# A hybrid attention and state-space layer: gate weights and decay rows loaded from GpSimd's queue, both directions' state products in one PSUM bank

## The chip, the cores and the metric

The kernel runs on one core of a Trainium2 chip. Its time is the device time of one execution in microseconds. Times are the median of several runs; the profile comes from one more execution. In the profile the engines are PE (TensorE matmul), PEld (TensorE weight load), DVE (VectorE), ACT (ScalarE), POOL (GpSimd) and SP (SyncE, which in this kernel issues every DMA).

## The reference

One layer on 512 latent tokens and 256 context tokens, width 2048, float32. Cut to what matters:

```python
shift, scale, gate = split(silu(c) @ w_mod + b_mod, 3)
px = (rmsnorm(x, norm_g) * (1 + scale) + shift) @ w_in     # latent
pc = (rmsnorm(ctx, norm_g) * (1 + scale_c) + shift_c) @ w_in
# attention: 16 heads of 64, 4 KV heads, window of 128 plus all context keys, sink, rotary
att = windowed_gqa(q, k, v, k_ctx, v_ctx, sink)
# state space: 16 heads of 64 in 4 groups, state 128, chunks of 128, forward and backward
u = silu(dwconv(xbc, conv_w, conv_b)); xs, B, C = split(u)
a_cs = cumsum(dt * a)                                       # per head and direction
y = (C B^T * exp(segsum(a_cs))) @ (dt * xs) + C @ state * exp(a_cs) + xs * d_skip
x = x + gate * concat(rmsnorm(att * silu(g)), rmsnorm(y * silu(z))) @ w_out
return rmsnorm(x, final_norm_g)
```

The vector `gate` (2048 numbers) is a product of one row, silu(c), with a 2048 x 2048 matrix. The states pass from chunk to chunk, from left to right for one direction and from right to left for the other; the context's final state is each direction's first.

## The kernel before, in words

Activations lie with the model width on the partitions, tokens along the free axis. Every projection is done in split precision: a weight tile is loaded as float32 (`wr`), ScalarE rounds it to `wh`, VectorE subtracts to get the rest `wl`, and TensorE adds three products (`mm` at L49 is the line of all of them). A unit is 128 output columns over 16 steps of k: `load_unit` loads it in two halves, each split in two quarters, and `proj` collects latent columns in the bank `pj` and, for units that context needs as well, context columns in `pjc`. Two buffers hold `wr`, four each hold `wh` and `wl`.

The stages in order: modulation and the z columns (to about 137 us), v and dt columns (to about 198), then units 1 to 16 in four groups of four (x, x, B, C columns of a state-space group), then k, q and g columns with attention (to about 861), then the output projection.

While the units of group g+1 run, the scan pieces of group g are put between their matmuls. `stream(g, i, mid)` gives `proj` a table of what to emit at which step k: `tokens(g)` at step 8 of the next group's first unit, `states(g)` after it, then `decay`, `state_term` and `back` for each pair of heads. The parts that matter here:

- `tokens` (L511): four matmuls give C B^T in a bank of the tag `tp`, VectorE makes the two masked copies `cb` from it (L521), and TensorE transposes xs and B into further `tp` banks (`xtp`, `btp`). The tag `tp` has two banks, so of three `xtp` in a row one needs the bank that `cb` reads.
- `states` (L544): for each of three steps and each of two directions, `xw` (VectorE), the product `stx` in a `tp` bank, and the update of `stt` on VectorE: first times `etot`, then plus the bank.
- `decay` (L574): for each head and direction the row of cumulated decays is broadcast from DRAM (`csd`) into `df` (four buffers; 128 partitions) and `ec` (two buffers; two heads of 64 partitions); ScalarE makes the exponentials, VectorE multiplies `df` with `cb`. `back` (L624) uses `df` in the product `yps`.
- `gate_step` (L280): the vector gate is computed on VectorE, 64 steps, one at each quarter of units 1 to 16. Step i multiplies a 128x512 weight tile `wg` with a column of silu(c) and adds it to `ga`. Weights are loaded two steps ahead into two buffers. After each 16 steps a matmul with ones sums over partitions, the row is stored to `grow`, and the only buffer of `ga` is set to zero by POOL (L289) for the next 16.

Instructions on each engine run in the order that a planner wrote at build time. It goes by program order, with blocks under `tc.high_priority` moved ahead by the number given, and by its own model of when an instruction is ready. `tc.issue_after(ld.ins)` orders an instruction behind the load `ld` on the same queue: the gate loads stand behind their unit's `wr` load on SP. A queue works in order: a load whose buffer is not free holds what stands behind it.

Of the kernel before, what the change touches and what calls it, by code (L numbers as in the profile page):

```python
# [14 lines left out]
P = 128  # L15
# [28 lines left out]
def emit(tc, xin, ctxT, wmod, wgate, bgate, wz, wvd, wu, wo, fng, vecs, cst, rope, out, dbg=None):  # L44
    nc = tc.nc
    es = ExitStack()

    def mm(o, l, r, start, stop):
        return nc.tensor.matmul(o, l, r, start=start, stop=stop)  # L49
# [4 lines left out]
    def tt(eng, o, a, b, op):  # L54
        eng.tensor_tensor(out=o, in0=a, in1=b, op=op)  # L55
# [7 lines left out]
    with es:  # L63
# [5 lines left out]
        def bank(tag, name, dt=F32, shape=(P, 512)):  # L69
            return ps.tile(list(shape), dt, tag=tag, name=name, bufs=pcount[tag])  # L70
# [200 lines left out]
        gacc, gw = [], []  # L271

        def gbuf(odd, name):
            if odd:
                return w2(name, "wg", 1)
            return wp.tile([P, 512], F32, tag="wg", name=name, bufs=GB)
# [3 lines left out]
        def gate_step(ld):  # L280

            i = next(gsteps, None)
            if i is None:
                return
            n, k = divmod(i, KT)
            if k == 0:
                ga = wp.tile([P, 512], F32, tag="ga", name=f"ga_{n}", bufs=1)
                gacc.append(ga)
                nc.gpsimd.memset(ga, 0.0)  # L289
                with tc.issue_after(ld.ins):  # L290
                    nc.sync.dma_start(ga[0:1, :], bgate[:, n * 512:(n + 1) * 512])
            ga = gacc[n]
            for ii in range(len(gw), min(i + 2, 4 * KT)):
                n_, k_ = divmod(ii, KT)
                gw.append(gbuf(ii % 2, f"wg_{n_}_{k_}"))
                with tc.issue_after(ld.ins):
                    nc.sync.dma_start(gw[ii], wgate[n_, k_])
            wg = gw[i]
            geng.scalar_tensor_tensor(out=ga, in0=wg, scalar=sc0[:, k:k + 1], in1=ga, op0=ALU.mult, op1=ALU.add)  # L299
            if k == KT - 1:  # L300
                gp = bank("tp", f"gp_{n}", shape=(1, 512))
                mm(gp, ones[:, 0:1], ga, True, True)
                nc.scalar.activation(ga[0:1, :], gp, AF.Copy)
                nc.sync.dma_start(grow[:, n * 512:(n + 1) * 512], ga[0:1, :])


        def load_unit(u, ctxp=False):

            for hf in range(2):
                with tc.high_priority(HP_W):  # L310
                    wr = wp.tile([P, 8, P], F32, tag="wr", name=f"wr_{u}_{hf}", bufs=WR)
                    ld = nc.sync.dma_start(wr, wu[u, :, hf * 8:hf * 8 + 8, :])
                for qf in range(2):
                    with tc.high_priority(HP_W):
                        wh = wp.tile([P, 4, P], F32R, tag="wh", name=f"wh_{u}_{hf}_{qf}", bufs=4)
                        rr = wr[:, qf * 4:qf * 4 + 4, :]
                        nc.scalar.activation(wh, rr, AF.Copy)  # L317
                        wl = wp.tile([P, 4, P], F32R, tag="wl", name=f"wl_{u}_{hf}_{qf}", bufs=4)
                        tt(nc.vector, wl, rr, f32(wh), ALU.subtract)
                    if 1 <= u < 17:  # L320
                        gate_step(ld)
                    for i in range(4):
                        yield hf * 8 + qf * 4 + i, wh[:, i, :], wl[:, i, :]

        def proj(u, with_ctx, mid=(), btag="mm"):

            a = bank("mm", f"pj_{u}")
            b = bank(btag, f"pjc_{u}", shape=(P, CT)) if with_ctx else None
            late = []
            for k, wh, wl in load_unit(u):  # L330
                s0, s1 = k == 0, k == KT - 1
                if k in mid:
                    mid[k]()
                mm(a, wh, xh[k], s0, False)
                mm(a, wh, xl[k], False, False)
                mm(a, wl, xh[k], False, s1)
                if with_ctx:
                    late.append((k, wh, wl))
                    if k % 4 == 3:
                        for kk, h, l in late:  # L340
                            mm(b, h, ch[kk], kk == 0, False)
                            mm(b, h, cl[kk], False, False)
                            mm(b, l, ch[kk], False, kk == KT - 1)
                        late = []
            return a, b
# [60 lines left out]
        z7, _ = proj(0, False)  # L406
# [12 lines left out]
        def w2(name, tag="w2", bufs=4, shape=(P, S)):  # L419
            return sd.tile(list(shape), F32, tag=tag, name=name, bufs=bufs)  # L420
# [4 lines left out]
        csd = dp.tile([32, S], F32, name="csd")  # L425
# [118 lines left out]
        def states(g):  # L544

            xtok, btok = G[g]["xtok"], G[g]["btok"]
            hs = slice(4 * g, 4 * g + 4)

            def xw(d, t):
                o = w2(f"xw_{g}_{d}_{t}", "xw", 2, (P, 4, HD))  # L550
                tt(nc.vector, o, xtok[:, t, :].rearrange("p (a b) -> p a b", a=4),
                   wdt[:, d, t, hs].unsqueeze(2).to_broadcast([P, 4, HD]), ALU.mult)
                return o.rearrange("p a b -> p (a b)")

            stt_ = [w2(f"stt_{g}_{d}", f"stt{d}", 1, (P, NT, 256)) for d in range(2)]
            for d in range(2):
                first = 0 if d == 0 else 3
                sp_ = bank("tp", f"stc_{g}_{d}", shape=(P, 256))
                mm(sp_, btok[:, 4, :], xw(d, 4), True, False)
                mm(sp_, btok[:, 5, :], xw(d, 5), False, True)  # L560
                nc.scalar.activation(stt_[d][:, first, :], sp_, AF.Copy)
            for stp in range(3):
                for d in range(2):
                    c = stp if d == 0 else 3 - stp
                    nx = c + 1 if d == 0 else c - 1
                    sp_ = bank("tp", f"stx_{g}_{d}_{c}", shape=(P, 256))
                    mm(sp_, btok[:, c, :], xw(d, c), True, True)
                    tt(nc.vector, stt_[d][:, nx, :].rearrange("p (a b) -> p a b", a=4),
                       stt_[d][:, c, :].rearrange("p (a b) -> p a b", a=4),
                       etot[:, d, c, hs].unsqueeze(2).to_broadcast([P, 4, HD]), ALU.mult)  # L570
                    tt(nc.vector, stt_[d][:, nx, :], stt_[d][:, nx, :], sp_, ALU.add)
            G[g]["stt"] = stt_

        def decay(g, pr):  # L574

            cb = G[g]["cb"]
            tix = 2 * g + pr
            ecs = [w2(f"ec_{tix}_{d}", "ec", 2) for d in range(2)]

            for d in range(2):  # L580
                with tc.high_priority(HB):
                    for hh in range(2):
                        nc.sync.dma_start(ecs[d][hh * 64:hh * 64 + 64], csd[d * 16 + tix * 2 + hh].partition_broadcast(64))
                nc.scalar.activation(ecs[d], ecs[d], AF.Exp)
            dm = []
            for hh in range(2):
                r = tix * 2 + hh
                dx = []
                for d in range(2):

                    df = w2(f"df_{r}_{d}", "df", DF)
                    with tc.high_priority(HB):
                        nc.sync.dma_start(df, csd[d * 16 + r].partition_broadcast(P))
                    for c in range(NT):
                        cc = slice(c * P, (c + 1) * P)
                        nc.scalar.activation(df[:, cc], df[:, cc], AF.Relu, bias=cs[:, d, c, r:r + 1], scale=-1.0)  # L596
                    nc.scalar.activation(df, df, AF.Exp, scale=-1.0)
                    for c in range(NT):
                        cc = slice(c * P, (c + 1) * P)
                        nc.scalar.activation(df[:, cc], df[:, cc], AF.Copy, scale=dtt[:, d, c, r:r + 1])  # L600
                    tt(nc.vector, df, df, cb[d], ALU.mult)
                    dx.append(df)
                tt(nc.vector, dx[0], dx[0], dx[1], ALU.add)
                dm.append(dx[0])
            G[g]["dec", pr] = dm, ecs
# [138 lines left out]
        for j in range(4):  # L744
            qs = []
            for i in range(2):
                a, _ = proj(U0 + 18 + 2 * j + i, False)
# [23 lines left out]
            for b in range(NT):  # L771
# [46 lines left out]
                for n, t in enumerate(kts):  # L818
                    tp = bank("tp", f"ptp_{j}_{b}_{n}")
# [18 lines left out]
            for jj in {0: (), 1: (0,), 2: (1,), 3: (2, 3)}[j]:  # L838
                for i in range(2):
                    t = 2 * jj + i  # L840
                    a, _ = proj(U0 + 26 + t, False)
# [233 lines left out]
```

## Time and profile before

| | |
|---|---|
| median of 3 runs | 1054.75 us (1053.28 to 1058.65) |
| the profiled execution | 1057.19 us, span 1055.4 us |
| granted TensorE clock, mean | 0.985 of full speed |
| busy: PE, PEld | 1012.8 us (96%), 818.6 us (78%) |
| busy: DVE, ACT, POOL | 693.2 us (66%), 538.6 us (51%), 141.4 us (13%) |
| gate weight loads `wg` | 64 of 256 KB, from SP |
| decay loads `df` and `ec` | 32 of 256 KB and 32 of 128 KB, from SP |
| unit weight loads `wr` | 70 of 512 KB, from SP |

"Busy" is the time in which an engine had an instruction under way; matmuls are pipelined, so a busy TensorE may still be short of its peak. A wait is idle time of an engine that ended when another one's instruction, or a DMA, released it. A row of the waits names the engine and line that waited, what released it, the total in microseconds, how many times, and the longest. A row of the order of time names start, duration, engine, line, the instruction, tiles as out<-in, and in brackets the idle time before it and its releaser.

### The profile page before, as it was taken

What the parts mean: (1) busy time and instruction counts of PE and PEld (TensorE: products, weight loads), DVE (VectorE), ACT (ScalarE), POOL (GpSimd) and SP (SyncE); (2) the same over time, 40 slices, a digit from 0 to 9 for tenths busy, and PEclk for the clock granted to TensorE, in tenths of its full rate; (3) what the DMA queues carried; (4) which work ended last, traced back from release to release, by engine and by line L of the source; (5) the groups of instructions that cost most, each with busy time, mean ns of one, the idle gap of its engine ahead of it and who ended that gap; (6) DMA issues with size and microseconds to landing.
All of it is one profiled execution on the core that took longest, in us unless ns stands there. A gap on an engine that the chain in (4) does not pass through costs nothing.

```text
span 1055.4 us, 15566 instructions
## 1 busy us (share of the span) xinstructions
PE 1012.8 (96%) x5682; PEld 818.6 (78%) x5682; DVE 693.2 (66%) x1346; ACT 538.6 (51%) x1236; POOL 141.4 (13%) x96
## 2 busy tenths in 40 slices
PE   5999999999999999999998899999999998999996
PEld 4676789888887787788876778777777777888885
DVE  4323378564875875775759888788797865333765
ACT  6222265255537637546645567575666654333333
POOL 0232300000000000000008000000000018644220
PEclk8999999999999999999999899999999998999999
DMA  9999964363534544534131211112111134442304
GB/s 330 383 343 348 341 213 124 101 196 110 170 121 150 160 130 150 157 122 141 61 106 60 80 41 61 41 40 81 40 60 56 45 142 187 141 167 88 106 29 160
DMA packets 53404, 147.31 MB, mean 140 GB/s; under 512 B 6056, under 2 KB 6568, under 8 KB 53072
## 3 DMA queue, kind: packets, MB, share of 16 engines
q1 hardware_dynamic: 53328, 146.31, 41.7%
q8 instruction: 45, 0.74, 0.3%
q14 instruction: 31, 0.25, 0.1%
HBM read 142.02 MB, written 4.27 MB: 139 GB/s over the span
## 4 chain that ended last, share of the span: by engine, by line
PE 59%; DVE 10%; DMA 8%; ACT 5%; issue 3%; POOL 1%; SPq 0%; ACTq 0%; DVEq 0%; POOLq 0%
PE pj L49 25%; PE o L49 14%; PE pjc L49 5%; PE pv L49 3%; PE ptp L821 3%; DMA wg<-in_wgate_dram 3%; PE sl L49 3%; DMA df<-csd 2%; DMA ec<-csd 2%; PE sc L49 2%; DVE wl L55 1%; DVE ga L299 1%; PE stx L49 1%; DVE df L55 1%; DVE ec L55 1%
## 5 line engine op out<-in xcount | busy, mean ns | idle before, releaser
L49 PE MATMUL pj<-xh,wl 128*128 128x512 f32 x560 | 225.7, 403 | 3.7 <-DVE wl L55 3.7
L49 PE MATMUL pj<-xh,wh 128*128 128x512 f32 x560 | 228.7, 408 | 0.5 <-ACT kT L701 0.5
L49 PE MATMUL pj<-xl,wh 128*128 128x512 f32 x560 | 226.0, 404 | 0.0
L317 ACT ACTIVATE wh<-wr 128x512 fp32r<-128x512 f32 x140 | 87.5, 627 | 125.0 <-PE pjc L49 79.0
L55 DVE TENSOR_TENSOR wl<-wr,wh 128x512 fp32r<-128x512 f32 x140 | 97.8, 700 | 43.6 <-ACT wh L317 42.8
L49 PEld LDWEIGHTS pj<-xh,wl 128*128 128x128 f32 x560 | 106.0, 189 | 26.2 <-DVE wl L55 4.6
L49 PEld LDWEIGHTS pj<-xh,wh 128*128 128x128 f32 x560 | 106.2, 190 | 23.8 <-ACT df L596 2.8
L49 PEld LDWEIGHTS pj<-xl,wh 128*128 128x128 f32 x560 | 106.1, 190 | 19.3
L55 DVE TENSOR_TENSOR wol<-wo,woh 128x512 fp32r<-128x512 f32 x56 | 54.3, 983 | 65.4 <-ACT woh L911 59.0
L55 POOL TENSOR_TENSOR hacc<-hacc,hsq 128x512 f32<-128x512 f32 x14 | 21.2, 1512 | 420.8 <-ACT hsq L719 420.6
L911 ACT ACTIVATE woh<-wo 128x512 fp32r<-128x512 f32 x56 | 34.7, 629 | 73.3 <-PE o L49 65.2
L299 DVE SCALAR_TENSOR_TENSOR ga<-wg,sc,ga 128x512 f32<-128x512 f32 x64 | 47.9, 748 | 36.5 <-DMA wg<-in_wgate_dram 36.3
L49 PE MATMUL pjc<-chq,wh 128*128 128x256 f32 x224 | 64.0, 286 | 0.7 <-DVE xs L487 0.7
L49 PE MATMUL pjc<-clq,wh 128*128 128x256 f32 x224 | 63.6, 284 | 0.0
L49 PE MATMUL pjc<-chq,wl 128*128 128x256 f32 x224 | 63.6, 284 | 0.0
L596 ACT ACTIVATE df<-df,cs 128x128 f32<-128x128 f32 x128 | 43.2, 391 | 29.1 <-DMA df<-csd 29.0
L825 ACT ACTIVATE ph<-ptp 128x512 fp32r<-128x512 f32 x72 | 41.1, 598 | 28.4 <-PE ptp L821 26.9
L49 PE MATMUL o<-woh,hsh 128*128 128x512 f32 x128 | 52.1, 407 | 3.1 <-ACT part L930 3.1
L55 DVE TENSOR_TENSOR pl<-ptp,ph 128x512 fp32r<-128x512 f32 x72 | 48.5, 684 | 8.2 <-ACT ph L825 8.0
L796 ACT ACTIVATE pe<-sl,nm 128x256 f32<-128x256 f32 (+1 forms) x64 | 33.7, 526 | 37.2 <-DVE nm L794 35.5
L49 PE MATMUL o<-wol,hsh 128*128 128x512 f32 x128 | 51.2, 400 | 0.0
L49 PE MATMUL o<-woh,hsl 128*128 128x512 f32 x128 | 51.1, 399 | 0.0
(274 smaller groups left out, 2296.4 us busy)
## 6 DMA issues: line engine op xcount, KB each, us to landing
wr<-in_wu_dram SPq DMA_DIRECT2D x70, 512.0 KB, 3.7
wm<-in_wmod_dram SPq DMA_DIRECT2D x64, 512.0 KB, 7.7
wg<-in_wgate_dram SPq DMA_DIRECT2D x64, 256.0 KB, 2.8
wo<-in_wo_dram SPq DMA_DIRECT2D x32, 512.0 KB, 4.8
df<-csd SPq DMA_DIRECT2D x32, 256.0 KB, 4.1
wsr<-in_wz_dram SPq DMA_DIRECT2D x16, 448.0 KB, 6.8
wr_v<-in_wvd_dram SPq DMA_DIRECT2D x16, 288.0 KB, 2.9
xt<-in_xin_dram SPq DMA_DIRECT2D x8, 512.0 KB, 8.4
```

The source lines that it names most:

```text
L49: return nc.tensor.matmul(o, l, r, start=start, stop=stop)
L55: eng.tensor_tensor(out=o, in0=a, in1=b, op=op)
L299: geng.scalar_tensor_tensor(out=ga, in0=wg, scalar=sc0[:, k:k + 1], in1=ga, op0=ALU.mult, op1=ALU.add)
L317: nc.scalar.activation(wh, rr, AF.Copy)
L596: nc.scalar.activation(df[:, cc], df[:, cc], AF.Relu, bias=cs[:, d, c, r:r + 1], scale=-1.0)
L796: nc.scalar.activation(pe[:, 0:nl * P], sl, AF.Exp, bias=nm[:, i:i + 1], accum_out=sm[:, i, 0:1])
L821: nc.tensor.transpose(tp[:, i * P:(i + 1) * P], pt[i][:, n * P:(n + 1) * P], ident)
L825: nc.scalar.activation(ph, tp, AF.Copy)
L911: nc.scalar.activation(wh, wr[:, i, :], AF.Copy)
```

## The change

Three edits. The loads of the gate weights are issued from GpSimd's queue and no longer ordered behind the unit's load (the load of the bias row into `ga` stays on SP behind it). The loads of `ec` and `df` are issued from GpSimd's queue. In `states` the products of both directions of one step share one PSUM bank, half each, in place of a bank for each.

```diff
@@ -293,8 +293,7 @@
             for ii in range(len(gw), min(i + 2, 4 * KT)):
                 n_, k_ = divmod(ii, KT)
                 gw.append(gbuf(ii % 2, f"wg_{n_}_{k_}"))
-                with tc.issue_after(ld.ins):
-                    nc.sync.dma_start(gw[ii], wgate[n_, k_])
+                nc.gpsimd.dma_start(gw[ii], wgate[n_, k_])
             wg = gw[i]
             geng.scalar_tensor_tensor(out=ga, in0=wg, scalar=sc0[:, k:k + 1], in1=ga, op0=ALU.mult, op1=ALU.add)
             if k == KT - 1:
@@ -560,10 +559,11 @@
                 mm(sp_, btok[:, 5, :], xw(d, 5), False, True)
                 nc.scalar.activation(stt_[d][:, first, :], sp_, AF.Copy)
             for stp in range(3):
+                sp2 = bank("tp", f"stx_{g}_{stp}", shape=(P, 2, 256))
                 for d in range(2):
                     c = stp if d == 0 else 3 - stp
                     nx = c + 1 if d == 0 else c - 1
-                    sp_ = bank("tp", f"stx_{g}_{d}_{c}", shape=(P, 256))
+                    sp_ = sp2[:, d, :]
                     mm(sp_, btok[:, c, :], xw(d, c), True, True)
                     tt(nc.vector, stt_[d][:, nx, :].rearrange("p (a b) -> p a b", a=4),
                        stt_[d][:, c, :].rearrange("p (a b) -> p a b", a=4),
@@ -580,7 +580,7 @@
             for d in range(2):
                 with tc.high_priority(HB):
                     for hh in range(2):
-                        nc.sync.dma_start(ecs[d][hh * 64:hh * 64 + 64], csd[d * 16 + tix * 2 + hh].partition_broadcast(64))
+                        nc.gpsimd.dma_start(ecs[d][hh * 64:hh * 64 + 64], csd[d * 16 + tix * 2 + hh].partition_broadcast(64))
                 nc.scalar.activation(ecs[d], ecs[d], AF.Exp)
             dm = []
             for hh in range(2):
@@ -590,7 +590,7 @@
 
                     df = w2(f"df_{r}_{d}", "df", DF)
                     with tc.high_priority(HB):
-                        nc.sync.dma_start(df, csd[d * 16 + r].partition_broadcast(P))
+                        nc.gpsimd.dma_start(df, csd[d * 16 + r].partition_broadcast(P))
                     for c in range(NT):
                         cc = slice(c * P, (c + 1) * P)
                         nc.scalar.activation(df[:, cc], df[:, cc], AF.Relu, bias=cs[:, d, c, r:r + 1], scale=-1.0)
```

## Rows read from the trace of the kernel before

**Rows 1.** Windows by round: us, busy us of each engine (instructions), granted clock, DMA share, GB/s.

```profile
266.00:346.00 80.00, 79.30 (x460) 66.47 (x460) 57.03 (x99) 44.89 (x107) 0.53 (x1) 1.00 0.45 142
346.00:425.00 79.00, 76.97 (x448) 64.19 (x447) 57.29 (x99) 46.71 (x113) 0.53 (x1) 1.00 0.49 149
425.00:507.00 82.00, 79.20 (x452) 66.30 (x452) 57.13 (x99) 47.00 (x113) 0.00 (x0) 0.98 0.45 137
```

**Rows 2.** Waits of TensorE, 198 to 552: total us, times, longest.

```profile
PE xtp L531 <- DVE cb L521: 4.3, 2, 2.5
PE yps L49 <- DVE df L55: 1.9, 1, 1.9
PE csp L49 <- DVE da L451: 1.5, 1, 1.5
```

**Rows 3.** Order of time, VectorE at 431: start us, us, line, tiles, [idle before].

```profile
428.42 0.75 DVE L299 SCALAR_TENSOR_TENSOR ga<-wg,sc,ga 128x512 f32<-128x512 f32 x1 [1.36 <-DMA wg<-in_wgate_dram]
431.38 0.75 DVE L299 SCALAR_TENSOR_TENSOR ga<-wg,sc,ga 128x512 f32<-128x512 f32 x1 [2.21 <-DMA wg<-in_wgate_dram]
...
432.65 1.28 DVE L521 SCALAR_TENSOR_TENSOR cb<-cbp,cs_sb 128x512 f32<-128x512 f32 x2
```

**Rows 4.** Order of time, VectorE at 351.

```profile
349.72 0.75 DVE L299 SCALAR_TENSOR_TENSOR ga<-wg,sc,ga 128x512 f32<-128x512 f32 x1 [1.34 <-DMA wg<-in_wgate_dram]
351.24 0.75 DVE L299 SCALAR_TENSOR_TENSOR ga<-wg,sc,ga 128x512 f32<-128x512 f32 x1 [0.77 <-DMA wg<-in_wgate_dram]
...
352.51 0.68 DVE L521 SCALAR_TENSOR_TENSOR cb<-cbp,cs_sb 128x512 f32<-128x512 f32 x1
```

**Rows 5.** Order of time, VectorE at 208.

```profile
208.46 0.75 DVE L299 SCALAR_TENSOR_TENSOR ga<-wg,sc,ga 128x512 f32<-128x512 f32 x1 [0.41 <-DMA wg<-in_wgate_dram]
...
211.57 0.42 DVE L451 SCALAR_TENSOR_TENSOR da<-dtt,expa 128x96 f32<-128x96 f32 x2
```

**Rows 6.** Order of time, ScalarE at 544.

```profile
544.35 1.28 ACT L596 ACTIVATE df<-df,cs 128x128 f32<-128x128 f32 x4 [1.93 <-DMA df<-csd]
```

**Rows 7.** Waits of SP's queue, 198 to 552: total us, times, longest.

```profile
SPq L312 <- DVE wl L55: 105.7, 31, 10.6
SPq L297 <- DVE ga L299: 34.7, 35, 3.2
```

**Rows 8.** Waits of ScalarE, 198 to 552.

```profile
ACT wh L317 <- PE pjc L49: 79.0, 29, 5.4
ACT df L596 <- DMA df<-csd: 29.0, 14, 4.4
```

**Rows 9.** The gate weights' tile: issue ns min/median/max, and landing.

```profile
L297 SPq DMA_DIRECT2D wg<-in_wgate_dram x64: 327/328/1092, 157.3 to 471.5; - x64
...
DMA to landing us min/median/max: 2.5/2.8/5.5
```

**Rows 10.** Order of time, POOL.

```profile
261.27 0.53 POOL L289 MEMSET ga<- 128x512 f32 x1 [123.79 <-DMA grow<-ga]
...
558.21 1.75 POOL L55 TENSOR_TENSOR hacc<-hacc,hsq 128x512 f32<-128x512 f32 x1
559.92 1.29 POOL L55 TENSOR_TENSOR hsl<-hfu,hsh 128x512 fp32r<-128x512 f32 x1
```

**Rows 11.** Waits of VectorE, 198 to 552.

```profile
DVE ga L299 <- DMA wg<-in_wgate_dram: 33.5, 25, 3.0
```

**Rows 12.** Windows after the wait at 431, columns as in rows 1.

```profile
434.00:436.00 2.00, 2.00 (x9) 2.00 (x10) 2.00 (x4) 0.61 (x2) 0.00 (x0) 0.50 0.99 313
436.00:438.00 2.00, 2.00 (x9) 1.59 (x8) 2.00 (x5) 0.98 (x2) 0.00 (x0) 0.79 0.76 224
```

**Rows 13.** Order of time, TensorE in the state products of one group.

```profile
366.51 0.67 PE L49 MATMUL stx<-xw,btok 128*128 128x256 f32 x2
...
368.12 0.67 PE L49 MATMUL stx<-xw,btok 128*128 128x256 f32 x2
```

**Rows 14.** Order of time, VectorE beside them.

```profile
367.22 0.42 DVE L55 TENSOR_TENSOR stt<-stt,stx 128x256 f32<-128x256 f32 x1
```

## The prediction

> **What bounds the kernel now.** I read the windows by stage first, then the waits of each engine in the stretch that the edits touch (198 to 552 us: the units of the state-space groups, with the scan pieces between them), then the order of time around each place where TensorE stands still. The windows show TensorE busy for 79.30 of 80, 76.97 of 79 and 79.20 of 82 us in the three rounds of that stretch [rows 1]; VectorE is busy for 57 us of each. So TensorE sets the time, and nothing that shortens another engine's work pays unless a wait of TensorE ends earlier. Its waits are few: 4.3 us in two waits of the transposes xtp for VectorE's cb, 1.9 us of yps for df, 1.5 us of csp for da [rows 2], 7.7 us together. That is the most that any edit here can give back, but for the clock after the longest of them (below).
>
> Those waits have one cause in common. At 431 us VectorE idles 1.36 and then 2.21 us in front of two gate steps, until their weights land; the two cb instructions, which depend on neither, stand behind them in VectorE's order, and TensorE's 2.5 us wait ends with them [rows 2, 3]. At 351 us it is the same with 1.34 and 0.77 us of idle [rows 4]; that wait is 4.3 - 2.5 = 1.8 us. At 208 us a gate step with 0.41 us of idle stands ahead of da [rows 5]. At 544 us ScalarE idles 1.93 us for the landing of the last decay row df, on which yps depends [rows 6].
>
> **Part 1: gate weights (64 loads) and decay rows (32 df, 32 ec) from POOL's queue.** What it removes: these loads no longer stand in SP's queue with the unit weights wr. What that frees is worth nothing by the rows. SP held at wr until VectorE had freed its buffer, 31 times and 105.7 us [rows 7], and yet ScalarE's split of wr has no wait for a landing: its long wait is 79.0 us for TensorE's pjc [rows 8], so wr is early. Nor are the gate loads late because SP was busy elsewhere: SP stood at a gate load, waiting for the gate step that frees its buffer, 35 times and 34.7 us [rows 7], with two buffers for the weights. POOL will stand at the same loads waiting for the same two buffers. Cover of the zero: wr's lead; if it were gone, each late wr would cost up to a landing, 2.8 us by the median of a gate load [rows 9].
>
> What it adds: a POOL instruction for each load in place of SP's 0.327 us issue, and another way to the landing, which takes 2.5 to 5.5 us, median 2.8, now [rows 9]. No DMA is issued by POOL in this trace, so I bound the added time of a load, d. From below: 2.5 - 2.8 = -0.3 us, if POOL's own queue lets a load land as the best one does now. From above: 5.5 - 2.8 = +2.7 us. Nearer rows: POOL's memset takes 0.53 us and its two-input adds and subtractions 1.29 to 1.75 us [rows 10]; less SP's 0.33 that is +0.2, and +1.0 to +1.4. I take d = +0.5, nearer to the memset, which is the only kind of POOL instruction in this stretch, and keep both ends.
>
> The Trainium skill ("DMA: Bandwidth & Descriptors", section "Latency and other measured facts") gives about 1 us to the first byte for a transfer issued from GpSimd and about 0.6 us from the sync and scalar queues. No run here shows it yet. By that page d would be an estimated +0.4 us, and the sum below +2.3 in place of +2.7.
>
> What queues behind a waiting load on POOL: other gate loads, df, ec and the memset of ga. The first three stood in one queue before as well, so their order among themselves costs nothing new. The memset waits for the landing of the store of grow (261.27 us, and two more like it) [rows 10] and can now hold a df; ScalarE, which waits for df, already idles 29.0 us there in 14 waits [rows 8] without TensorE's rows showing it except at 544 us. I put it at nothing; without that cover it is three times a landing, 8 us. POOL's next work is the sums of squares at 558 us [rows 10], after the last df, whose wait ends at 544.35 [rows 6], so nothing of that is held.
>
> What lies on the path, with d = 0.5: the second gate step ahead of cb starts 0.5 later at 351 and at 431 us, and TensorE's wait grows by as much: 2 x 0.5 = 1.0. The gate step ahead of da: 0.5. The last df ahead of yps: 0.5. The other waits of VectorE for gate weights (25 in all, 33.5 us [rows 11]) grow too, but lie beside TensorE's unit work: 0.
>
> Then the clock. After the 2.5 us wait the granted clock falls to 0.50 for 434 to 436 and 0.79 for 436 to 438 us [rows 12], that is to the lower level, 1.2 GHz, and back to 2.4: 2 x 0.50 + 2 x 0.21 = 1.4 us lost. After the 1.8 us wait at 351 the whole round's mean is 1.00 [rows 1]. With +0.5 this wait comes to 2.3 us, between the two, so I count half of 1.4: 0.7.
>
> **Part 2: gate loads no longer issued after the unit's own load.** Nothing ties them to it on POOL. The planner may start each round's 16 steps earlier; it can't go past a round, since ga has one buffer, and its memset waits for the grow store [rows 10]. I put it at 0; what another order could do is the rival below.
>
> **Part 3: both directions' state products in one bank.** Six banks per group become three. If an access to one half holds the other half back, the second direction's product must wait for the first one's add. Rows: stx at 366.51, its add from 367.22 for 0.42 us, next stx at 368.12 [rows 13, 14]. The next one already starts 0.48 us after that add has ended: cost 0, with TensorE's unit matmuls between as cover. Without it, each of 12 steps costs up to 368.12 - 367.25 = 0.9 us if the planner puts the two side by side: 11 us at worst. From below: all of TensorE's idle for stx, which has no row among its main waits, so 0.
>
> **Sum:** 1.0 + 0.5 + 0.5 + 0.7 = +2.7 us. Against the profiled execution: 1057.19 (span 1055.4 and 1.8 around it) to 1059.9. That execution is 2.4 us above the median of the runs, 1054.75, so the median goes to 1057.5. With d at its bounds the four places and the clock give -1.2 to about +15 (4 x 2.7 + 3 x 1.4).
>
> **Rivals.**
> *The order turns in favour.* A planner that knows the loads to be elsewhere puts cb, and da, ahead of the gate steps. Then the 1.8 and 2.5 us waits go and 1.4 us of clock with them: -5.7; with da's 1.5 too, -7.2: 1047.6 to 1049. For: both waits come from the order alone, cb needs nothing that the gate step makes. Against: the same two pieces of program text still bring them together, and gate steps that are freed from the unit's load can come earlier, right into the same place.
> *Late landings (slower).* One mechanism: VectorE in order, behind a gate step whose weights land later. Decides from d = 0.65 us: 4 x 0.65 + 2 x 1.4 = 5.4, as two of the waits then come to 2.5 us, the one that drew the clock down. At d = 1.2, the middle of POOL's adds less SP's issue: 4 x 1.2 + 3 x 1.4 = +9.0: 1063.8. From d = 1.8 VectorE binds whole rounds: 57 busy + 33.5/4 = 8.4 of gate waits + 8 pairs x 1.8 = 80 us, the round; at d = 2 it is 1.4 us more in each of three rounds: 8.0 + 4.2 + 4.2 = +16: 1071. For: POOL's adds. Against: the memset.
> *The bank makes TensorE wait:* half a microsecond in each of 12 steps, +6: 1060.8. For: one bank, two engines. Against: the 0.48 us in hand.
> *It does not do what it says:* POOL's loads land as SP's do and the order stays: 1054.8, within 1.
>
> **How the numbers follow.** Forecast (d from 0 to 0.65, the order as it is) 0.33; order in favour 0.27; late landings 0.28; bank 0.04; no effect 0.08. Time: 1057.5. Within 0.5% (5.3 us, about what a measurement of this kernel can tell from no change): 0.31 of the forecast, 0.08 and 0.01 of late landings: 0.40. Faster: 0.27. Slower: 0.27 + 0.04 + 0.02 = 0.33. The range holds the order's -7.2 and late landings up to d near 2: 1046 to 1069; the forecast's own is 1054.8 to 1060.
>
> **What would show it.** d: the landing of wg beside today's 2.8 us, and VectorE's waits for wg beside 33.5 us in 25. Order: whether the gate steps with idle time in front still stand right ahead of cb near 351 and 431 us; if TensorE's waits for cb are gone, the rival is right. Clock: a granted clock under 1.00 in the round from 346 us on says that the longer wait drew it down. Bank: waits of TensorE's stx for an add. Wrong altogether if ScalarE's split waits for wr, or if time moves outside 198 to 592 us.

## The result and the profile after

The kernel after takes 1065.97 us (median of 9 runs, 1059.40 to 1069.05) beside 1054.98 us of the kernel before (9 runs, 1051.88 to 1058.65): a ratio of 1.0092, 95% interval [1.0066, 1.0118], slower. The profiled execution's span is 1064.2 us, 8.8 more than before. The loss arises ahead of the last pair's product yps, which starts at 558.97 us in place of 549.73.

TensorE's waits in the same units, now 198 to 562 us (total us, times, longest), answer to [rows 2]:

```profile
PE xtp L530 <- DVE cb L520: 5.0, 3, 2.6
PE pjc L49 <- DVE xs L486: 4.9, 4, 2.4
PE yps L49 <- DVE df L55: 2.6, 1, 2.6
PE csp L49 <- DVE da L450: 1.6, 1, 1.6
PE stc L49 <- DVE xw L55: 1.3, 2, 1.1
PE stx L49 <- DVE xw L55: 0.8, 1, 0.8
```

The waits of [rows 2] grew by 0.7, 0.7 and 0.1 us. The large item is one that did not stand there: pjc for xs. The same view of the kernel before has it at 0.7 us in three waits:

```profile
PE pjc L49 <- DVE xs L487: 0.7, 3, 0.3
PE stc L49 <- DVE xw L55: 0.5, 1, 0.5
PE stx L49 <- ACT stt L561: 0.3, 1, 0.3
```

So pjc adds 4.2 us; stc and stx add 1.3. No late gate load stands right ahead of these two: the gate steps before the stc wait at 287 us had no idle time in front, and the stx wait at 530 us comes after the last gate step (479.9 us). All six together: 16.2 - 9.2 = 7.0 us. The window of the middle round (us, busy of each engine, granted clock, DMA share, GB/s) beside [rows 1]:

```profile
346.00:425.00 79.00, 74.47 (x419) 62.16 (x418) 54.50 (x95) 41.24 (x101) 16.18 (x30) 0.96 0.44 137
```

It has a granted clock of 0.96 where it had 1.00, the rounds on both sides have 1.00 and 0.98 as before: 79 x 0.04 = 3.2 us. It comes in two pieces, behind the wait for cb at 353 us (2.0 us) and behind the pjc wait at 392 us (2.4 us). Windows there, same columns:

```profile
353.00:356.00 3.00, 1.03 (x7) 0.79 (x5) 3.00 (x6) 0.60 (x1) 0.54 (x1) 0.89 0.36 120
356.00:358.00 2.00, 2.00 (x10) 1.82 (x10) 1.15 (x2) 0.85 (x2) 0.54 (x1) 0.50 0.98 336
358.00:360.00 2.00, 2.00 (x9) 1.59 (x9) 2.00 (x6) 0.61 (x2) 0.54 (x1) 0.82 0.29 94
...
396.00:398.00 2.00, 2.00 (x8) 1.65 (x8) 2.00 (x4) 1.37 (x2) 0.40 (x1) 0.57 0.62 205
398.00:400.00 2.00, 2.00 (x7) 1.55 (x6) 0.78 (x2) 0.00 (x0) 0.14 (x1) 0.58 0.82 262
```

Both times the clock goes to the lower level, 1.2 GHz, and back: 3 x 0.11 + 2 x 0.50 + 2 x 0.18 = 1.7 us at the first, 2 x 0.43 + 2 x 0.42 = 1.7 at the second. In the kernel before, the wait at 351 us was 1.8 us long and its round kept 1.00 [rows 1]. Waits and clock, 7.0 + 3.2 = 10.2 us, come near the 8.8 us and the 1.7 us that the kernel after is ahead as the stretch begins (da starts at 209.85 us, before at 211.57 [rows 5]).

The loads of the gate weights' tile (issue ns min/median/max; landing), beside [rows 9]:

```profile
L296 POOL DMA_DIRECT2D wg<-in_wgate_dram x64: 538/538/715, 136.6 to 476.1; - x64
...
DMA to landing us min/median/max: 2.7/3.2/6.8
```

The gate weights' landing went from 2.8 to 3.2 us in the median, the slowest from 5.5 to 6.8. What the late ones did is plain on VectorE, around 233 and 392 us (start us, us, line, tiles, [idle before]):

```profile
232.99 1.54 DVE L298 SCALAR_TENSOR_TENSOR ga<-wg,sc,ga 128x512 f32<-128x512 f32 x2 [2.89 <-DMA wg<-in_wgate_dram]
...
235.22 0.75 DVE L486 SCALAR_TENSOR_TENSOR xs<-pj,v_sb,xs 128x511 f32<-128x511 f32 x1
...
386.73 0.75 DVE L298 SCALAR_TENSOR_TENSOR ga<-wg,sc,ga 128x512 f32<-128x512 f32 x1 [2.30 <-DMA wg<-in_wgate_dram]
...
391.93 0.75 DVE L298 SCALAR_TENSOR_TENSOR ga<-wg,sc,ga 128x512 f32<-128x512 f32 x1 [3.86 <-DMA wg<-in_wgate_dram]
...
393.92 0.74 DVE L486 SCALAR_TENSOR_TENSOR xs<-pj,v_sb,xs 128x511 f32<-128x511 f32 x1
```

The convolution of xs reads the bank of pj, and TensorE's next context products start only as the second of its steps on pj (L486) has ended, at 236.12 and 394.81 us. It stands behind gate steps in VectorE's order, and these stand still for 2.89 and 3.86 us. In the kernel before, a gate step ahead of xs at 386 us had already idled 2.86 us, and TensorE waited 0.2 us there. What came ahead of the load for the step at 391.93 on POOL's queue:

```profile
383.46 1.04 POOL L583 DMA_DIRECT2D ec<-csd  x2
384.49 0.57 POOL L593 DMA_DIRECT2D df<-csd  x1
385.06 0.54 POOL L296 DMA_DIRECT2D wg<-in_wgate_dram  x1
387.77 0.54 POOL L296 DMA_DIRECT2D wg<-in_wgate_dram  x1 [2.17 <-DVE ga L298]
```

The load issued at 385.06 follows two ec and one df without a gap, and lands only as the step starts, 391.93 - 385.06 = 6.9 us later. The row at 387.77 shows another small part of the delay: the step that frees its buffer ended at 386.73 + 0.75 = 387.48, so POOL started 0.29 us after the release. Its other gate loads that waited for a gate step started 0.29 to 0.30 us after it; on SP it was 0.03 us (a step ended at 224.14, the next load started at 224.17).

### The profile page after: what moved, and what is told of

The parts are those of the page before. It is cut to its first block, busy times and chain, and to the rows that moved or that the text cites. A ratio compares the mean times of both kernels' runs of the same rounds, so it can differ in the third digit from the quotient of the medians.

```text
span 1064.2 us, 15597 instructions
## 1 busy us (share of the span) xinstructions
PE 1014.7 (95%) x5682; PEld 821.4 (77%) x5682; DVE 693.6 (65%) x1346; ACT 538.2 (51%) x1236; POOL 209.8 (20%) x224
## 4 chain that ended last, share of the span: by engine, by line
PE 41%; DVE 4%; ACT 2%; issue 2%; DMA 1%; POOL 1%; SPq 0%; ACTq 0%; POOLq 0%
PE pj L49 15%; PE o L49 14%; PE pv L49 3%; PE ptp L821 3%; PE sl L49 3%; PE sc L49 2%; DMA wo<-in_wo_dram 1%; DVE wl L55 0%; POOL hal L55 0%; PE pjc L49 0%; DVE kr L55 0%; DVE hfu L722 0%; DMA df<-csd 0%; DVE krt L55 0%; DVE kl L55 0%
## 5 line engine op out<-in xcount | busy, mean ns | idle before, releaser
L296 POOL DMA_DIRECT2D wg<-in_wgate_dram x64 | 34.8, 543 | 198.5 <-DVE ga L298 116.1
L298 DVE SCALAR_TENSOR_TENSOR ga<-wg,sc,ga 128x512 f32<-128x512 f32 x64 | 47.9, 748 | 31.5 <-DMA wg<-in_wgate_dram 30.9
L596 ACT ACTIVATE df<-df,cs 128x128 f32<-128x128 f32 x128 | 43.3, 391 | 35.7 <-DMA df<-csd 33.4
L55 POOL TENSOR_TENSOR wsl<-wsr,wsh 128x896 fp32r<-128x896 f32 x16 | 33.9, 2117 | 100.9 <-ACT wsh L231 95.6
```

The lines of the kernel that those rows point to most:

```text
L296: nc.gpsimd.dma_start(gw[ii], wgate[n_, k_])
```

## The experiments

Twelve kernels, each timed in five rounds against the kernel before. The theories of the first four: **A**, gate weights land late; **B**, decay rows land late; **C**, the shared bank; **D**, the loss arises only where both kinds of load share POOL's queue.

**e1_gate_only**: the kernel before with the gate loads alone moved.

```diff
-                with tc.issue_after(ld.ins):
-                    nc.sync.dma_start(gw[ii], wgate[n_, k_])
+                nc.gpsimd.dma_start(gw[ii], wgate[n_, k_])
```

> The gate weights alone go to POOL; decay rows stay on SP, banks as before. Theory A (late gate weights: each load starts 0.3 us after its buffer is free in place of 0.03 and lands in 3.2 in place of 2.8 us, VectorE stands in order behind it): +6 us or more of the changed kernel's +10, so 1061 to 1066 us, with waits of TensorE for xs and cb of 9 us or more. Theory B (late decay rows): 1053 to 1057. Theory C (the shared bank): 1053 to 1057. Theory D (only all loads together on one POOL queue, gate loads behind decay rows): 1054 to 1058, with no gate load over 5.5 us to its landing.

Measured: 1064.85 us (1061.23 to 1067.61), ratio 1.0086 [1.0063, 1.0109]. Its waits of TensorE, 198 to 562 us:

```profile
PE pjc L49 <- DVE xs L486: 7.0, 3, 4.6
PE stc L49 <- DVE xw L55: 4.5, 3, 1.8
```

The gate loads alone make a loss as large as the whole change, and at xs and the state products (stc), not at cb (1.3 us here). A's time holds; the waits for xs and cb are 8.3 us together, where it asked for 9 or more.

**e2_rows_only**: the decay rows alone moved.

```diff
-                        nc.sync.dma_start(ecs[d][hh * 64:hh * 64 + 64], csd[...].partition_broadcast(64))
+                        nc.gpsimd.dma_start(ecs[d][hh * 64:hh * 64 + 64], csd[...].partition_broadcast(64))
...
-                        nc.sync.dma_start(df, csd[d * 16 + r].partition_broadcast(P))
+                        nc.gpsimd.dma_start(df, csd[d * 16 + r].partition_broadcast(P))
```

> The decay rows alone go to POOL. Theory A: 1053 to 1058, the waits of VectorE for gate weights as before (about 33 us in 25). Theory B: 1061 to 1066, with ScalarE's waits for df and ec over 40 us and TensorE's wait for yps near 2.6 us. Theory C: 1053 to 1057. Theory D: 1054 to 1058.

Measured: 1075.03 us (1069.61 to 1078.29), ratio 1.0177 [1.0148, 1.0206]: twice the loss of the whole change, and 9 us above the range of B, which had the way right. The order of time of POOL and of SP in this run:

```profile
218.56 1.72 POOL L583 DMA_DIRECT2D ec<-csd  x3 [80.90 <-DVE wdt L55]
...
221.35 1.65 POOL L593 DMA_DIRECT2D df<-csd  x3
```

```profile
219.35 1.11 SPq L297 DMA_DIRECT2D wg<-in_wgate_dram  x2
```

Eight row loads (4 of 128 KB, 4 of 256 KB, 1.5 MB) leave POOL in 4.4 us, beside two gate loads on SP. In the kernel before, the same eight left SP over 13.3 us, with six gate loads between them (the first and the last rows):

```profile
217.73 0.52 SPq L583 DMA_DIRECT2D ec<-csd  x1
...
229.65 1.33 SPq L593 DMA_DIRECT2D df<-csd  x3
```

In the kernel after, POOL's queue spaces them too: 216.34 to 229.14 us, again with gate loads between. From 222 to 230 us the DMA engines' mean busy share is 1.00 in e2, 0.86 before and 0.84 after. The two engines that wait for loads in e2, VectorE and then ScalarE:

```profile
226.74 1.54 DVE L299 SCALAR_TENSOR_TENSOR ga<-wg,sc,ga 128x512 f32<-128x512 f32 x2 [4.80 <-DMA wg<-in_wgate_dram]
```

```profile
225.47 0.63 ACT L584 ACTIVATE ec<-ec 128x512 f32<-128x512 f32 x1 [4.26 <-DMA ec<-csd]
```

Gate loads that were not moved land late too (median 3.2 us, as in the kernel after), and TensorE waits 8.2 us for xs and 7.8 us for cb.

**e3_bank_only**: the shared bank alone.

```diff
+                sp2 = bank("tp", f"stx_{g}_{stp}", shape=(P, 2, 256))
...
-                    sp_ = bank("tp", f"stx_{g}_{d}_{c}", shape=(P, 256))
+                    sp_ = sp2[:, d, :]
```

> The shared bank alone. Theories A, B and D: within 2 us of before, 1053 to 1057. Theory C: 1058 or more, with waits of TensorE for stx and stc of 2 us or more in all; the forecast had put the bank at nothing.

Measured: 1055.17 us (12 runs), ratio 1.0001 [0.9986, 1.0016]. The bank is worth nothing; C falls.

**e4_gate_back**: the kernel after with the gate loads back on SP (rows on POOL, shared bank).

```diff
-                nc.gpsimd.dma_start(gw[ii], wgate[n_, k_])
+                with tc.issue_after(ld.ins):
+                    nc.sync.dma_start(gw[ii], wgate[n_, k_])
```

> The changed kernel with the gate weights back on SP behind the unit's load; decay rows on POOL, one bank. Theory A: falls back to 1054 to 1058. Theory B: stays at 1062 to 1067. Theory C: 1058 or more. Theory D: 1054 to 1058, as gate loads and decay rows no longer share a queue.

Measured: 1073.38 us (1072.02 to 1074.90), ratio 1.0166 [1.0143, 1.0189], as e2 and above the range of every theory. To put the gate loads into the queue that holds the rows takes back some 8 us of the rows' loss, the reverse of D. A and B are each true alone, and they do not add.

The next four ask whether late gate weights are the cause or the order of the steps.

**n1_before_two_loads** and **n2_after_two_loads**: gate weights are loaded for the first two steps, the others use these tiles again.

```diff
                 gw.append(gbuf(ii % 2, f"wg_{n_}_{k_}"))
+                if ii > 1:
+                    gw.append(gw[ii - 2])
+                    continue
```

(The two lines stand ahead of the `append` that makes a new buffer.)

> The kernel before, with only the first 2 of the 64 gate weight loads left; the later gate steps multiply the same two tiles (the gate vector is left wrong by that; nothing else changes). VectorE then never waits for gate weights (33.5 us in 25 waits before). Theory 'late landings cost TensorE': the two waits of xtp for cb (4.3 us) and csp for da (1.5) shrink or go and the clock drop after 431 us with them: 1047 to 1051. Theory 'order' (the gate steps stand ahead of cb whether or not they idle, 0.75 us each): 1053 to 1055, as before.

> The kernel after, with the same cut: 2 gate weight loads in place of 64; decay rows on GpSimd's queue, shared bank. Theory 'late gate weights' (the loss of the change is VectorE idle at gate steps ahead of conv's xs and cb): within 2 us of the cut kernel before, 1047 to 1052. Theory 'rows late of themselves' (df and ec from GpSimd's queue land later and ScalarE and yps wait): 4 us or more above the cut kernel before. Theory 'order': 1062 to 1066, as the kernel after. If the rows alone (which cost 20 us) hurt only by taking DMA time from gate loads, their cost is gone here too.

Measured: n1 1050.67 us, ratio 0.994 [0.992, 0.996]; n2 1056.28 us, 1.0002 [0.9988, 1.0016]. Gate loads cost the kernel before 5.4 us (1056.05 beside them) and the kernel after about 10. The remaining difference, 5.6 us, is the rows' own: half the size of the whole loss, with hardly a gate load left. The main waits of n1's and of n2's TensorE:

```profile
PE xtp L534 <- DVE cb L524: 1.9, 2, 1.8
```

```profile
PE xtp L533 <- DVE cb L523: 5.8, 2, 2.9
```

and of their ScalarE:

```profile
ACT df L599 <- DMA df<-csd: 32.6, 15, 4.3
```

```profile
ACT df L599 <- DMA df<-csd: 48.9, 18, 6.1
```

With no gate load in the way, ScalarE waits 16 us longer for df, and the convolution of cT, from which cb comes, is late with it. pjc for xs is no longer among the main waits of either.

Of n1's two waits for cb, the later one fell from 2.5 to 0.2 us, but the one at 351 us is still 1.8 us long, though no load is late. VectorE's order there has six gate steps between the convolution of cT and cb, where the kernel before has four, and five of them run without a gap:

```profile
345.45 3.90 DVE L302 SCALAR_TENSOR_TENSOR ga<-wg,sc,ga 128x512 f32<-128x512 f32 x5
...
349.87 1.28 DVE L524 SCALAR_TENSOR_TENSOR cb<-cbp,cs_sb 128x512 f32<-128x512 f32 x2
```

So at this place the gate steps' own time holds cb as long as the late weights did: 'order' is right here, 'late landings' at the later one.

**v1_before_early_sum** and **v2_after_early_sum**: the sum that closes a round is planned earlier, so that the gate steps spread.

```diff
-                gp = bank("tp", f"gp_{n}", shape=(1, 512))
-                mm(gp, ones[:, 0:1], ga, True, True)
...
+                with tc.high_priority(HP_W):
+                    gp = bank("tp", f"gp_{n}", shape=(1, 512))
+                    mm(gp, ones[:, 0:1], ga, True, True)
...
```

> The kernel before, with the closing sum of each round of 16 gate steps (the matmul with ones, its copy and its store to grow) planned ahead of its place, so that the single ga is set to zero earlier and the next round's gate steps spread over the units in place of standing close together at its start. Theory 'bunched gate steps are what lands late': TensorE's waits for cb (4.3 us) go, 1047 to 1052. Theory 'a gate load lands late wherever other loads compete': waits move to other places, 1053 to 1058.

> The kernel after, with the same early sum. Theory 'bunched gate steps': VectorE's waits for gate weights (30.9 us in 20) halve, and the stalls of pjc for xs (4.9 us) and xtp for cb (5.0) go: 1052 to 1058. Theory 'competing loads': 1062 to 1068, as the kernel after. A planned order that puts more gate steps ahead of cb than before would make it slower than 1068.

Measured: v1 1057.93 us, 1.0018 [1.0003, 1.0032]; v2 1076.15 us, 1.0178 [1.0154, 1.0203]. In v1 cb's waits fall to 2.1 us, but the early sum itself now waits for the last gate step; in v2 the transposes' and cT's waits come instead:

```profile
PE gp L49 <- DVE ga L299: 2.9, 3, 1.8
```

```profile
PE xtp L531 <- DVE cb L521: 7.4, 3, 3.6
PE cbp L49 <- DVE cT L110: 6.0, 2, 3.1
```

In v2 gate steps with 3.28 and 3.62 us of idle in front (356 and 441 us) stand ahead of the convolution of cT. The time of v2 lies above both ranges, as the last sentence of what was expected allows, with cT in the place of cb. To spread the steps without choosing what stands behind them gains nothing.

The last four choose the place, and part the rows.

**s1_before_one_unit_later** and **s2_after_one_unit_later**: the 64 gate steps at units 2 to 17.

```diff
-                    if 1 <= u < 17:
+                    if 2 <= u < 18:
```

> The kernel before, with the 64 gate steps at units 2 to 17 in place of 1 to 16: the same loads and sums, but a round of 16 ends at the first unit of a group instead of its last, so that in VectorE's order no gate step stands between the convolution of cT and cb, nor around the convolution of the third unit (pj, pjc for xs). Theory 'a late gate load costs only where cb or xs stands behind it': TensorE's waits for cb (4.3 us) go and 4 to 6 us are won, 1049 to 1052, near the kernel with 2 gate loads (1050.7). Theory 'gate loads cost wherever they stand, by taking DMA time from the rest': 1054 to 1057, as before.

> The kernel after, with the same shift of the gate steps by one unit. Theory 'a late gate load costs only where cb or xs stands behind it': the loss of 10 us falls to that of the kernel after with 2 gate loads, 1054 to 1058. Theory 'competing loads wherever they stand': 1063 to 1068, as the kernel after.

Measured: s1 1049.20 us (1045.80 to 1052.05), ratio 0.9931 [0.9904, 0.9957]: this version beats both kernels. s2 stays at 1067.41 us, 1.0098 [1.0068, 1.0129], which its first theory had at 1054 to 1058: a miss, within the range of the second. In s1, a row each of TensorE's and of VectorE's waits:

```profile
PE xtp L531 <- DVE cb L521: 0.5, 2, 0.3
```

```profile
DVE ga L299 <- DMA wg<-in_wgate_dram: 29.5, 24, 3.7
```

VectorE idles for gate weights almost as long as before (29.5 beside 33.5 us [rows 11]), its gate loads even land later (median 3.6 us beside 2.8), and the wait for cb is all but gone, as no gate step stands between the convolution of cT and cb:

```profile
420.53 0.69 DVE L110 SCALAR_TENSOR_TENSOR cT<-cve,cT 128x512 f32<-128x512 f32 x1 [1.63 <-ACT cve L109]
421.57 0.69 DVE L55 TENSOR_TENSOR wl<-wr,wh 128x512 fp32r<-128x512 f32 x1 [0.35 <-ACT wh L317]
423.47 0.69 DVE L55 TENSOR_TENSOR wl<-wr,wh 128x512 fp32r<-128x512 f32 x1 [1.21 <-ACT wh L317]
424.08 1.28 DVE L521 SCALAR_TENSOR_TENSOR cb<-cbp,cs_sb 128x512 f32<-128x512 f32 x2
```

This is the clearest evidence here that the place decides, and not the sum of the waits; the order of the other steps changed with it. In s2 VectorE's row is 29.5 us in 24 as well, but TensorE stands elsewhere, and ScalarE with it:

```profile
PE cbp L49 <- DVE cT L110: 7.9, 3, 3.3
```

```profile
ACT df L596 <- DMA df<-csd: 50.4, 15, 11.1
```

One of these waits for df, 9.31 us, ends at 408.55 us. That df was issued from POOL's queue at 402.74 us, right behind gate loads that had waited for their gate steps until 400.90 and 402.22, and ScalarE started on it 5.8 us later. TensorE has no wait near this place; its nearest one for cT ends at 433 us (2.2 us). That the delay of ScalarE reaches cT is argued, and not shown.

**m1_two_loads_df** and **m2_two_loads_ec**: n1 with only df, or only ec, from POOL's queue.

```diff
-                        nc.sync.dma_start(df, csd[d * 16 + r].partition_broadcast(P))
+                        nc.gpsimd.dma_start(df, csd[d * 16 + r].partition_broadcast(P))
```

(m2 has the same edit on the load of `ec` instead.)

> The kernel before with 2 gate weight loads (1050.7 us; gate vector wrong by that), and of the change only the loads of df on GpSimd's queue. What is told apart is the 5.6 us between this cut kernel before and the cut kernel after. Theory 'df lands later and ScalarE's steps on it stand ahead of the convolution and of cb': 1054 to 1057. Theory 'ec, whose issue stands behind df in POOL's order and whose ScalarE step held cT at 421 us': 1050 to 1052.

> The same cut kernel before, and of the change only the loads of ec on GpSimd's queue (gate vector wrong by the 2 loads). Theory 'df lands later': 1050 to 1052. Theory 'ec': 1054 to 1057. If neither this nor the run with df alone is above 1053, it takes both in one queue.

Measured: m1 1062.97 us, 1.0066 [1.0040, 1.0092], 12 us above n1; m2 1053.74 us, 0.9974 [0.9955, 0.9992], 3 above n1. df is the dear one, more than expected, and again df alone costs more than df and ec together (n2, 5.6). ScalarE in m1, and the same place in n1:

```profile
226.15 0.99 ACT L599 ACTIVATE df<-df,cs 128x128 f32<-128x128 f32 x3 [3.11 <-DMA df<-csd]
228.54 0.63 ACT L587 ACTIVATE ec<-ec 128x512 f32<-128x512 f32 x1 [1.40 <-DMA ec<-csd]
...
233.27 0.63 ACT L587 ACTIVATE ec<-ec 128x512 f32<-128x512 f32 x1 [1.58 <-DMA ec<-csd]
...
234.39 0.76 ACT L487 ACTIVATE xs<-pj,v_sb 128x512 f32<-128x512 f32 x1
```

```profile
229.88 0.99 ACT L599 ACTIVATE df<-df,cs 128x128 f32<-128x128 f32 x3 [1.64 <-DMA df<-csd]
...
231.29 0.76 ACT L487 ACTIVATE xs<-pj,v_sb 128x512 f32<-128x512 f32 x1
```

The xs step of ScalarE starts 3.1 us later, behind 3.11 + 1.40 + 1.58 = 6.1 us of idle for landings (n1: 1.64 here and 1.37 for one ec before it), and TensorE has a wait of 3.1 us for xs. But ScalarE's order differs as well: more steps on df stand ahead of xs in m1. Landing and order both have a part, and this pair does not say how large each is.

## Why the prediction was right and wrong

The time fell into the range, 8.5 us above the forecast. The rival "late landings" comes nearest: VectorE in order, behind a gate step whose weights land later. But its sum at d = 0.65 was 5.4 us, half of the 11.0 us measured, and the place that cost most, xs, is not among its four. That the range held is in part luck: its upper end was drawn for d near 2 at those four places, and here d was some 0.7.

- **TensorE bounds, and the loads ahead of other work in VectorE's and ScalarE's order are the cause:** right, for cb at 431 us and for xs. At 351 us the gate steps' own time does as much (n1). s1 gains 0.7% by an edit that changes only where the gate steps stand.
- **What SP is spared is worth 0:** right. SP now stands mostly at wr, 312.2 us in 35 waits, and ScalarE's split of wr still has no wait for a landing among its rows.
- **The added time d = +0.5:** the landing gave +0.4 in the median, and the start after the release 0.29 us in place of 0.03, so some +0.7. That is about the rival's turning point (0.65). The +0.4 is not the queue's alone: with every gate load on SP the median is 3.6 us in s1 and 4.4 in v1. The shortest landing is 2.5 to 2.6 us from SP and 2.7 from POOL in every run with all 64 loads. The estimate of +0.4 from the Trainium skill ("DMA: Bandwidth & Descriptors", "Latency and other measured facts") agrees with the landing's median in the kernel after, but not with the shortest landings, which are 0.1 to 0.2 us apart, and the measured figures decide; the start after a wait is not in it.
- **cb 1.0, da 0.5, yps 0.5:** measured 0.7, 0.1 and 0.7; the sum 1.5 where 2.0 was said. At its two places cb grew by only 0.2 and 0.1 us, with three gate steps ahead of it in place of four; 0.4 us is a new wait at 275 us.
- **"The other waits of VectorE for gate weights grow too, but lie beside TensorE's unit work: 0":** this is the step that failed. VectorE's sum did not even grow (30.9 us in 20 beside 33.5 in 25), but the longest went from 3.0 to 3.9 us, and two of the long ones fell ahead of xs: 4.2 us at pjc. In the kernel before, gate steps stood ahead of xs as well and had 0.7 us of TensorE's waits, which I did not count as a place that was about to decide. e1 shows it alone (7.0 us), n1 and n2 without gate loads have it no more.
- **The clock, +0.7:** right in kind, too small. The wait for cb at 351 us grew from 1.8 to 2.0 us, by less than the 0.5 forecast, and behind it the clock fell all the same: 1.7 us lost there, and as much again behind the new wait for xs at 392.
- **"Their order among themselves costs nothing new":** wrong as a rule. e2, e4 and m1 lose more than the kernel after or n2, so it matters which loads share a queue and what is issued beside them; in m1 the order of ScalarE's steps changes as well. I had looked for a turned order on VectorE alone; there it moved by one gate step ahead of cb.
- **The memset that can hold a df, at 0; ScalarE's 29.0 us for df grow to 33.4:** in the kernel after TensorE's only row from it is the 0.7 at yps. But the nothing fails too: without gate loads the moved rows cost 5.6 us (n2 beside n1), with 48.9 us of ScalarE's waits for df in place of 32.6, and TensorE's waits for cb rise from 1.9 to 5.8 us. How much of the kernel after's loss is theirs stays open.
- **The bank, 0:** right (e3).

What stays open: why rows alone cost 19 us and rows with gate loads 10, and df alone 12 and df with ec 5.6. In both pairs two queues issue at the same moment what one queue had spaced, which fits the burst of e2 (4.4 us, and 12.8 in the kernel after); but the planner's order changes with each edit, and no run holds it still.

## What to carry to other kernels

A late load costs the bounding engine only where its next work stands behind the waiting instruction on another engine: list every such place, also those whose wait is now near zero, because here a few tenths of a microsecond turned one into the largest item. In this kernel loads in one queue spaced each other, and rows moved alone left in a burst; test each kind alone and together. A side job in fixed steps can be moved against the main job's phases: here one unit's shift won 0.7%, with the same loads and nearly the same waits of VectorE.

## What the runs showed of the hardware

- A load from POOL's queue occupies POOL for 0.54 us (SP: 0.33 [rows 9]), and starts 0.29 to 0.30 us after the step that frees its buffer (SP: 0.03).
- Gate loads that stayed on SP landed later when other loads moved to POOL: median 2.8 to 3.2 us in e2. But the median moves without such a move as well, to 4.4 us in v1, and the time does not follow it: v1 is 0.2% slower than the kernel before, s1 with 3.6 us 0.7% faster.
- Between a wait of TensorE of 1.8 us, behind which the granted clock stayed at 1.00, and one of 2.0 us at the same place, behind which it fell to 0.50, lie 1.7 us of lost time, some eight times the 0.2 us of waiting. The length alone does not decide: behind the wait for xs at 233 us, also 2.0 us, the clock stayed at 1.00 (236 to 240 us).
